# Every second block of u multiplied as plain float32 while the heads are routed, and the tokens scaled in place

## The chip, the core and the metric

The kernel runs on one core of one Trainium2 chip. The metric is the device time of one execution in microseconds (us). A core has five engines with a queue of instructions each: TensorE (PE, with its weight loads shown as PEld), VectorE (DVE), ScalarE (ACT), GpSimd (POOL) and SyncE (SP), which here only issues DMAs. Each queue runs in its own order; semaphores make an instruction wait for another engine.

## What is computed

Two transformer-like blocks on 256 tokens of width 1024. The change lies in the last part, the expert layer of the second block (PEER):

```python
q = (xf @ w_q).reshape(n_tok, 8, 256)                      # 8 heads, keys of 2 x 128
s1 = einsum("thd,hnd->thn", q[..., :128], sub_keys[:, 0])  # and s2 with the other half
v1, i1 = top_k(s1, 16); v2, i2 = top_k(s2, 16)             # routing: 16 experts a head and token
idx, gates = ...top_k(v1 + v2)..., softmax(vals)
act = gelu(einsum("chkd,cd->chk", u[idx], xc))             # u: 16384 x 1024
out = einsum("chk,chkd->cd", act * gates, v[idx])
```

The kernel does not gather for most tokens: it multiplies all 16384 rows of u with 224 of the 256 tokens, in 128 blocks of 128 experts, and spreads the gates over the experts. The last 32 tokens (`GT`) are done by fetching the chosen rows of u and v.

## The kernel before

Products that must be as exact as float32 are made of three matmuls in the reduced form fp32r (`mm3`, line 209): an operand is split into a rounded part (hi, made by an ACT cast) and its remainder (lo, by a subtraction on DVE or POOL), and hi·hi, hi·lo and lo·hi are added up in PSUM.

The part at issue, in program order:

- `finish` (lines 1062 to 1074) adds the last residual to `h` and makes `hT`, the tokens transposed (128 x 1024 for each of two tiles c of 128 tokens), times a gain, but not yet times each token's scale `r4[c]`, which `row_scale` computes meanwhile on ACT and POOL.
- `scores(c, hd)` (lines 1236 to 1249): 16 plain float32 matmuls of `hT[c]` with the head's query weights (line 1241), 4 records of line 1247 with the sub keys, and an ACT copy that multiplies by `r4[c]`. A plain float32 matmul appears in the trace as two MATMUL records.
- Lines 1255 to 1262: the scaled tokens `t` are made on DVE from `hT` and a PSUM tile that holds r4 along the free side (`over_free`, line 318), then split into `x3` (`xuh`, `xul`).
- Lines 1264 to 1273: `hg`, the rows of the last 32 tokens, four copies of each, by one DVE operation on 128 x 1024 and two plain float32 matmuls with 512 columns (line 1272).
- `load_e` (lines 1279 to 1290) loads one block of u into a tile `er` (three of these, 512 KB each), casts its halves to `eh` on ACT (line 1286) and makes the remainders `el` (line 1288) on DVE and POOL in turn (`OPT["ulo"]`) until routing is over, and then on DVE alone (`ulo2`). There are four tiles each of `eh` and `el`, two blocks' worth.
- The loop over the 128 blocks (line 1366 on): 8 x `mm3` with 224 columns into `us`, gelu by ACT into `W`. At every fourth block `choose` routes one head of one token tile, a chain of some 30 small DVE operations whose last but one is line 1133, and `scores` makes the scores of a head three or four further on. From the fifth routed head, `fetch` (POOL, line 1322) brings 128 chosen rows of u and `take` (DVE, line 1329) multiplies them with `hg`. When all heads are routed, `weights` makes the gates, and `spread` (lines 1337 to 1360) puts them into `W`.
- For token tile 1, a route ends with a small DMA of the indices (`gidx`, line 1137) in SP's queue, the queue that also issues all loads of `er`.

A scheduler that works from a model of the engines puts the instructions of each engine in their final order; names with a number (`rt_5316`) are tiles.

Of the kernel before, what the change touches and what calls it, by code (L numbers as in the profile page):

```python
# [17 lines left out]
FT = mybir.dt.float32  # L18
# [5 lines left out]
AF = mybir.ActivationFunctionType  # L24
OP = mybir.AluOpType
AX = mybir.AxisListType

P = 128
T = 256
D = 1024  # L30
KT = D // P
# [5 lines left out]
GT = 32  # L37
ND = T - GT
# [7 lines left out]
TILED = ("w_in", "w_out", "w_ple_proj", "w_mlp_up", "w_mlp_down", "w_ple_gate", "w_in_2", "w_out_2", "peer_w_q_2")  # L46
DBG = None
MARK = None
PRI = dict(mix=20000, tail=20000, wt=20000, chain=20000, taps=20000, evac=40000, route=20000)
OPT = dict(lo='VVG', olo='V', mlo='V', clo='G', ulo='VG', ulo2='V', vlo='V', spr='SV', eraw=3, ring1=4, ring2=2, stag=3)  # L50


# [19 lines left out]
def body(ctx: ExitStack, tc: tile.TileContext, A, out, plan):  # L72
    nc = tc.nc
    V, S, G, PE = nc.vector, nc.scalar, nc.gpsimd, nc.tensor
# [22 lines left out]
    def bc(ap, n):  # L97
        return bass.AP(tensor=ap.tensor, offset=ap.offset, ap=[[0, P], [1, n]])
# [4 lines left out]
    scratch = pool(ctx, "scratch", 2)  # L103
# [15 lines left out]
    h = []  # L119
    for c in range(2):  # L120
        t = resid.tile([P, D], FT, name=f"h{c}")
        h.append(t)

    ident = consts.tile([P, P], FT, name="ident")
# [12 lines left out]
    def mm(shape=(P, 512)):  # L137
        return pmm.tile(list(shape), FT, name="mm", tag="mm")
# [67 lines left out]
    def mm3(ps, a, b, start, stop):  # L206

        for i, (x, y) in enumerate(((a[0], b[0]), (a[0], b[1]), (a[1], b[0]))):
            r = PE.matmul(ps, x, y, start=start and i == 0, stop=stop and i == 2)  # L209
        return r  # L210
# [105 lines left out]
    def over_free(r_, np_=P, c0=0, ps=None):  # L316

        return PE.matmul(ps[:, c0:c0 + np_], r_[:np_].to_broadcast([np_, P]), ident[:np_, :np_], start=True, stop=True)
# [4 lines left out]
    def over(ap, n=4):  # L323
        return ap[:, None, :].to_broadcast([P, n, P])
# [3 lines left out]
    def rows_(c):  # L328
        return slice(c * P, (c + 1) * P)
# [401 lines left out]
    with ExitStack() as mx:  # L731
# [29 lines left out]
        for c in C:  # L761
            ps = pacc.tile([P, 2, 512], FT, name=f"dn{c}")
# [473 lines left out]
    def scores(c, hd):  # L1236
        qh = scratch.tile([P, 2, P], FT, name="qh", tag="sq")
        ps = mm((P, 2, P))
        for b in range(2):
            for k in range(KT):  # L1240
                PE.matmul(ps[:, b, :], wq[hd](k, rows_(b)), hT[c][:, k, :], start=k == 0, stop=k == KT - 1)  # L1241
        S.copy(qh, ps)
        ps = mm((P, 2, P))
        sc = sc_[:, nsc[0] % 4]
        nsc[0] += 1
        for s in range(2):
            PE.matmul(ps[:, s, :], qh[:, s, :], skT[:, hd * 2 + s, :], start=True, stop=True)
        S.activation(sc, ps, AF.Copy, scale=r4[c])
        return sc

    order = [(1, hd) for hd in (0, 1, 2, 4, 6, 3, 5, 7)] + [(0, hd) for hd in (2, 4, 6, 3, 5, 7)]
    sc1 = [scores(*order[n]) for n in range(2)]


    for c, n in ((0, P), (1, ND - P)):
        ps = mm()
        over_free(r4[c], ps=ps)
        t = eraw.tile([P, KT, P], FT, name="er", tag="er")
        V.tensor_tensor(t, hT[c], over(ps[:, :P], KT), op=OP.mult)
        ts = slice(c * P, c * P + n)  # L1260
        S.copy(x3[0][:, :, ts], t[:, :, :n])
        V.tensor_tensor(x3[1][:, :, ts], t[:, :, :n], x3[0][:, :, ts].bitcast(FT), op=OP.subtract)

    hg = pr.tile([P, D], FT, name="hg")
    hn = eraw.tile([P, D], FT, name="er", tag="er")
    nc.sync.dma_start(hn, bc(A["norm_ffn_g_2"], D))
    V.scalar_tensor_tensor(hn, h[1], r4[1], hn, op0=OP.mult, op1=OP.mult)
    sel = scratch.tile([P, P], FT, name="sel", tag="sq")
    V.tensor_copy(sel.rearrange("p (b t) -> p b t", t=GT), ident[:, None, P - GT:].to_broadcast([P, 4, GT]))
    for n in range(2):  # L1270
        pt = mm()
        PE.matmul(pt, sel, hn[:, n * 512:(n + 1) * 512], start=True, stop=True)
        S.copy(hg[:, n * 512:(n + 1) * 512], pt)
    ag, gg = pr.tile([P, 32], FT, name="ag"), pr.tile([P, 32], FT, name="gg")
    sc1 += [scores(*order[n]) for n in range(2, 4)]

    ne = [0]

    def load_e(src, i, pat):

        raw = eraw.tile([P, D], FT, name="er", tag="er")
        nc.sync.dma_start(raw, src)
        hi, lo = [[esplit.tile([P, 512], FR, name="e" + x, tag="e" + x) for _ in range(2)] for x in "hl"]
        for n in range(2):
            r_ = raw[:, n * 512:(n + 1) * 512]
            S.copy(hi[n], r_)  # L1286
            e = V if pat[ne[0] % len(pat)] == "V" else G
            e.tensor_tensor(lo[n], r_, hi[n].bitcast(FT), op=OP.subtract)  # L1288
            ne[0] += 1
        return hi, lo  # L1290
# [69 lines left out]
            S.copy(W[:, at:, ts], ip[:, at:, :])  # L1360

    mark("u")
    uq = [load_e(A["u"][0], 0, OPT["ulo"])]
    p1 = None
    nr, nsp, nf, ps = 0, 0, 0, None
    for i in range(NB):
        p_ = i // 2
        if i + 1 < NB:
            uq.append(load_e(A["u"][i + 1], i + 1, OPT["ulo"] if p1 is None else OPT["ulo2"]))
        uh, ul = uq.pop(0)  # L1370
        if i % 2 == 0:
            ps = pu.tile([P, 2, T], FT, name="us", tag="us")[:, :, :ND]
        for k in range(KT):
            ks = rows_(k % 4)
            mm3(ps[:, i % 2, :], (uh[k // 4][:, ks], ul[k // 4][:, ks]), (x3[0][:, k, :], x3[1][:, k, :]), k == 0, k == KT - 1)
        if i % 2 == 0:
            continue
        ib = slice(i - 1, i + 1)
        nt = 4 * nsp
        if nt < ND:  # L1380
            S.activation(W[:, ib, nt:], ps[:, :, nt:], AF.Gelu_apprx_tanh)
        if nt:
            g_ = scratch.tile([P, 2, T], FT, name="ga", tag="sq")
            S.activation(g_[:, :, :nt], ps[:, :, :nt], AF.Gelu_apprx_tanh)
            V.tensor_tensor(W[:, ib, :nt], W[:, ib, :nt], g_[:, :, :nt], op=OP.mult)
        if nr >= 5 and p_ < 26 or p1 is not None and (todo or nf < 32):
            if len(todo) == 2 or nf == 32 and todo:
                take()
            if nf < min(32, 16 if nr < 8 else 32):
                fetch("peer_u_2", nf)  # L1390
                nf += 1
        if p_ == 25:
            while todo:
                take()
        if nr < len(order) and p_ % 2 == 0:
            choose(*order[nr], sc1[nr])
            nr += 1
            if nr + 3 < len(order):
                sc1.append(scores(*order[nr + 3]))
            if nr == len(order):  # L1400
                weights()
                more_rows()
                p1 = p_ + 1
        elif nr == len(order):
            want = -(-ND // 4 * (p_ + 1 - p1) // (64 - p1))
            while nsp < want:
                spread(nsp, i + 1, OPT["spr"][nsp % len(OPT["spr"])])
                nsp += 1
# [106 lines left out]
```

## Time and profile before

| | us |
|---|---|
| median of 3 runs | 1417.33 (1414.58 to 1418.09) |
| the profiled execution | 1420.28 |
| its span, first to last instruction | 1418.4 |
| mean granted TensorE clock | 0.974 of full |
| routing and u, first score to the last product of u | 563.27 to 1067.92 |

The profiled execution is 2.95 us above the median, and 1.9 us of it lie outside the span. The stage at issue covers 505 us, 36% of the span; the v products follow it.

### The profile page before, as it was taken

Reading aid. Unit: us, or ns where it says so; the run is one execution under the profiler, and the core shown is the slowest. Engines: PE = TensorE matmul, PEld = TensorE weight load, DVE = VectorE, ACT = ScalarE, POOL = GpSimd, SP = SyncE. Lnnn points to the kernel's source line nnn. Section 1 sums busy time; section 2 is a strip of 40 time slices with the busy share of each in tenths; the row PEclk is TensorE's granted clock in tenths of the full one; section 3 lists DMA queues with packets and bytes.
Section 4 is the critical chain, followed back from the end, with each engine's and each line's share of the span. In section 5 each row is a group of like instructions: output and inputs, shape, how many; then the busy total and the mean of one; then the engine's idle time right before and its main releaser. Section 6 shows DMA issues by size and latency. Waiting matters only on the chain.

```text
span 1418.4 us, 25628 instructions
## 1 busy us (share of the span) xinstructions
PE 1325.7 (93%) x9602; PEld 1250.2 (88%) x9602; DVE 1085.3 (77%) x2205; ACT 745.8 (53%) x1422; POOL 295.2 (21%) x278
## 2 busy tenths in 40 slices
PE   5999999999998969698899899999999999999997
PEld 5989979998878958598899899999998899899997
DVE  4978948765557986889987977888886676777765
ACT  5785356444454433243444566776665554555554
POOL 2520012000004851136434620000000121221000
PEclk9999999999999979899999999999999999999999
DMA  7533045655636500738546884544456778777773
GB/s 268 167 122 120 19 168 197 200 183 186 189 117 224 177 15 3 281 113 290 164 157 192 290 263 156 161 161 155 151 165 196 249 267 271 270 262 256 218 210 116
DMA packets 72780, 261.30 MB, mean 184 GB/s; under 512 B 9024, under 2 KB 9408, under 8 KB 71760
## 3 DMA queue, kind: packets, MB, share of 16 engines
q1 hardware_dynamic: 62432, 224.82, 48.1%
q0 software_dynamic: 9216, 33.56, 7.3%
q8 instruction: 75, 1.23, 0.4%
q10 hardware_dynamic: 1008, 1.30, 0.3%
q14 instruction: 49, 0.40, 0.1%
HBM read 258.56 MB, written 1.05 MB: 183 GB/s over the span
## 4 chain that ended last, share of the span: by engine, by line
PE 69%; DVE 18%; DMA 7%; ACT 3%; issue 3%; POOL 0%; ACTq 0%; DVEq 0%; POOLq 0%
PE us L209 18%; PE mm L209 18%; PE dn L209 6%; PE vacc L1437 5%; PE mm L1437 5%; DMA er<-in_peer_v_dram 4%; DVE el L1288 4%; PE mm L1355 3%; PE vacc L1435 3%; PE mm L1435 2%; DVE cfp L1024 2%; PE mm L1241 2%; ACT eh L1286 1%; DMA rows<-in_peer_u_dram,gidx 1%; DVE cv L390 1%
## 5 line engine op out<-in xcount | busy, mean ns | idle before, releaser
L1286 ACT CAST eh<-er 128x512 fp32r<-128x512 f32 x512 | 311.1, 619 | 331.1 <-PE us L209 141.1
L1288 DVE TENSOR_TENSOR el<-er,eh 128x512 fp32r<-128x512 f32 x457 | 321.7, 724 | 133.0 <-ACT eh L1286 131.0
L209 PE MATMUL us<-xuh,el 128*128 128x224 f32 x1024 | 284.7, 278 | 18.8 <-DVE el L1288 12.9
L209 PE MATMUL us<-xuh,eh 128*128 128x224 f32 x1024 | 288.0, 281 | 1.8 <-ACT eh L1286 1.8
L209 PE MATMUL us<-xul,eh 128*128 128x224 f32 x1024 | 283.4, 277 | 0.0
L209 PEld LDWEIGHTS us<-xuh,el 128*128 128x128 f32 x1024 | 198.9, 194 | 22.2 <-DVE el L1288 15.4
L193 ACT CAST wh<-w 128x1024 fp32r<-128x1024 f32 (+1 forms) x142 | 147.7, 1050 | 130.5 <-PE mm L209 75.6
L209 PEld LDWEIGHTS us<-xuh,eh 128*128 128x128 f32 x1024 | 199.2, 194 | 2.1 <-ACT eh L1286 2.1
L199 DVE TENSOR_TENSOR wl<-w,wh 128x1024 fp32r<-128x1024 f32 (+1 forms) x110 | 135.4, 1237 | 84.3 <-ACT wh L193 84.1
L209 PEld LDWEIGHTS us<-xul,eh 128*128 128x128 f32 x1024 | 199.2, 195 | 0.0
L1437 PE MATMUL vacc<-w,eh 128*128 128x448 f32 x508 | 167.2, 375 | 0.0
L1437 PE MATMUL mm<-w,eh 128*128 128x448 f32 x508 | 167.2, 375 | 0.0
L1435 PE MATMUL vacc<-w,el 128*128 128x224 f32 x512 | 137.8, 269 | 4.9 <-DVE el L1288 4.4
L1322 POOL DMA_INDIRECT rows<-in_peer_v_dram,gidx x32 | 49.0, 1532 | 428.6 <-DVE hg L1331 248.7
L1435 PE MATMUL mm<-w,el 128*128 128x224 f32 x512 | 135.5, 265 | 0.0
L209 PE MATMUL mm<-xTh,wh 128*128 128x256 f32 x416 | 118.9, 286 | 14.0 <-ACT wh L193 13.9
L209 PE MATMUL mm<-xTl,wh 128*128 128x256 f32 x416 | 118.6, 285 | 0.6 <-DVE xTl L253 0.6
L209 PE MATMUL mm<-xTh,wl 128*128 128x256 f32 x416 | 118.4, 285 | 0.0
L1435 PEld LDWEIGHTS vacc<-w,el 128*128 128x128 f32 x512 | 98.0, 191 | 11.2 <-DVE el L1288 11.0
L203 POOL TENSOR_TENSOR wl<-w,wh 128x512 fp32r<-128x512 f32 (+1 forms) x64 | 87.2, 1389 | 83.7 <-ACT wh L193 83.6
L1437 PEld LDWEIGHTS mm<-w,eh 128*128 128x128 f32 x508 | 95.3, 188 | 7.2
L1437 PEld LDWEIGHTS vacc<-w,eh 128*128 128x128 f32 x508 | 95.5, 188 | 6.8
(421 smaller groups left out, 2800.1 us busy)
## 6 DMA issues: line engine op xcount, KB each, us to landing
er<-in_u_dram SPq DMA_DIRECT2D x128, 512.0 KB
er<-in_peer_v_dram SPq DMA_DIRECT2D x128, 512.0 KB
w<-in_w_in_dram SPq DMA_DIRECT2D x48, 512.0 KB
w<-in_w_mlp_up_dram SPq DMA_DIRECT2D x32, 512.0 KB
w<-in_w_mlp_down_dram SPq DMA_DIRECT2D x32, 512.0 KB
w<-in_w_out_dram SPq DMA_DIRECT2D x16, 512.0 KB
W<-in_peer_w_q_dram SPq DMA_DIRECT2D x6, 1024.0 KB
w<-in_w_ple_gate_dram SPq DMA_DIRECT2D x8, 512.0 KB
```

The source lines that it names most:

```text
L193: S.copy(hi, t)
L199: V.tensor_tensor(lo, t, hi.bitcast(FT), op=OP.subtract)
L203: G.tensor_tensor(lo[s_], t[s_], hi[s_].bitcast(FT), op=OP.subtract)
L209: r = PE.matmul(ps, x, y, start=start and i == 0, stop=stop and i == 2)
L1024: V.scalar_tensor_tensor(cf[:, b, :] if k == 30 else part, uc[:, b, k:k + T], wk_, part, op0=OP.mult, op1=OP.add)
L1241: PE.matmul(ps[:, b, :], wq[hd](k, rows_(b)), hT[c][:, k, :], start=k == 0, stop=k == KT - 1)
L1286: S.copy(hi[n], r_)
L1288: e.tensor_tensor(lo[n], r_, hi[n].bitcast(FT), op=OP.subtract)
L1322: G.indirect_dma_start(out=rw, out_offset=None, in_=A[name][0], in_offset=bass.IndirectOffsetOnAxis(ap=gidx[:, n % 32:n % 32 + 1], axis=0))
L1355: PE.matmul(ps[:, k, :], wj[:, k, :], one[:, k, :], start=True, stop=True)
L1435: PE.matmul(acc[b][:, :ND], vl[n][:, bs], wi[:, :ND], start=False, stop=False)
L1437: PE.matmul(acc[b], vh[n][:, bs], wi, start=False, stop=i == NB - 1)
```

## The change

1. Blocks 0, 2, 4, ... 50 of u are no longer split: their raw tile `er` is the weight operand of 8 plain float32 matmuls with 224 columns of `hT` (new line 1378).
2. The other blocks are as before, but all their remainders are made on DVE: POOL has none left.
3. The scaled tokens are written over `hT` itself, under a priority `xu` (new lines 1253 to 1260); the scores are taken from the scaled `hT`, so their copy no longer scales.
4. The rows `hg` (`by_rows`) are made after block 9 and no longer ahead of block 0.

```diff
-        S.activation(sc, ps, AF.Copy, scale=r4[c])
+        S.copy(sc, ps)
...
-    sc1 = [scores(*order[n]) for n in range(2)]
-
-
-    for c, n in ((0, P), (1, ND - P)):
-        ps = mm()
-        over_free(r4[c], ps=ps)
-        t = eraw.tile([P, KT, P], FT, name="er", tag="er")
-        V.tensor_tensor(t, hT[c], over(ps[:, :P], KT), op=OP.mult)
-        ts = slice(c * P, c * P + n)
-        S.copy(x3[0][:, :, ts], t[:, :, :n])
-        V.tensor_tensor(x3[1][:, :, ts], t[:, :, :n], x3[0][:, :, ts].bitcast(FT), op=OP.subtract)
+
+    with tc.high_priority(offset=PRI["xu"]):
+        for c, n in ((0, P), (1, ND - P)):
+            ps = mm()
+            over_free(r4[c], ps=ps)
+            V.tensor_tensor(hT[c], hT[c], over(ps[:, :P], KT), op=OP.mult)
+            ts = slice(c * P, c * P + n)
+            S.copy(x3[0][:, :, ts], hT[c][:, :, :n])
+            V.tensor_tensor(x3[1][:, :, ts], hT[c][:, :, :n], x3[0][:, :, ts].bitcast(FT), op=OP.subtract)
+    sc1 = [scores(*order[n]) for n in range(4)]
...
-    def load_e(src, i, pat):
+    def load_e(src, i, pat, exact=False):
 
         raw = eraw.tile([P, D], FT, name="er", tag="er")
         nc.sync.dma_start(raw, src)
+        if exact:
+            return raw, None
...
-            uq.append(load_e(A["u"][i + 1], i + 1, OPT["ulo"] if p1 is None else OPT["ulo2"]))
+            uq.append(load_e(A["u"][i + 1], i + 1, OPT["ulo2"], p1 is None and i + 1 < 52 and (i + 1) % 4 in (0, 2)))
...
+            if ul is None:
+                PE.matmul(ps[:, i % 2, :], uh[:, rows_(k)], hT_[:, k].rearrange("p c t -> p (c t)")[:, :ND], start=k == 0, stop=k == KT - 1)
+                continue
             mm3(ps[:, i % 2, :], (uh[k // 4][:, ks], ul[k // 4][:, ks]), (x3[0][:, k, :], x3[1][:, k, :]), k == 0, k == KT - 1)
...
+        if p_ == 4:
+            by_rows()
```

How the queues stand there. On PE at the start of u, before: the scores of two heads (lines 1241 and 1247), the two rows of r4 (line 318), the product for hg (line 1272), a third head, then block 0 as fp32r.

```order
L1241 MATMUL mm<-hT,wq 128x128 x16
L1247 MATMUL mm<-skT,qh 128x128 x2
L1241 MATMUL mm<-hT,wq 128x128 x16
L1247 MATMUL mm<-skT,qh 128x128 x2
L318 MATMUL mm<-ident,r_5513 128x128
L318 MATMUL mm<-ident,r_5624 128x128
L1272 MATMUL mm<-er,sel 128x512 x2
L1241 MATMUL mm<-hT,W 128x128 x16
L209 MATMUL us<-xuh,eh 128x224
```

The same place after the change; line 1066 is the transposes of `finish`, line 1378 the plain products of u.

```order
L1066 MATMUL mm<-ident,h_86 128x128 x5
L318 MATMUL mm<-ident,r_5513 128x128
L1066 MATMUL mm<-ident,h_86 128x128 x3
L318 MATMUL mm<-ident,r_5624 128x128
L1241 MATMUL mm<-hT,wq 128x128 x16
L1378 MATMUL us<-hT,er 128x224 x8
L209 MATMUL us<-xuh,eh 128x224
L209 MATMUL us<-xul,eh 128x224
L1378 MATMUL us<-hT,er 128x224 x2
L1247 MATMUL mm<-skT,qh 128x128 x2
```

The rows of r4 have moved ahead of the first score, the first block of u stands behind that score, and line 1272 (now 1274) is gone from here.

On DVE ahead of the first score, after the change: the second route (lines 1104 to 1114, on `rt`) with the scaling (line 1257, second tile) in its middle and the split (line 1260) behind it.

```order
L1108 MAX_INDEX rt_5316<-rt_5316 128x8
L1114 TENSOR_TENSOR rt_5316<-rt_5316 128x120
L1108 MAX_INDEX rt_5316<-rt_5316 128x8
L1113 TENSOR_SCALAR rt_5316<-rt_5316 128x16
L1257 TENSOR_TENSOR hT<-hT,mm 128x8x128
L1104 MAX rt_5316<-rt_5316 128x8
L1105 MAX_INDEX rt_5316<-rt_5316 128x8
L1106 MATCH_REPLACE rt_5316<-rt_5316 128x136
L1260 TENSOR_TENSOR xul<-hT,xuh 128x8x96
```

Before, the scaling stood one route later, behind the same line 1104 of the third route; all of the second route's rows up to line 1133 were ahead of it.

On POOL from the first block of u, before: remainders of u (line 1288) and fetches (line 1322) mixed.

```order
L1149 COPY r_5624<-rr 128x1
L1288 TENSOR_TENSOR el<-er,eh 128x512 x9
L1322 DMA W<-in_peer_u_dram,gidx 128x1024 x4
L1288 TENSOR_TENSOR el<-er,eh 128x512 x2
L1322 DMA W<-in_peer_u_dram,gidx 128x1024 x3
L1288 TENSOR_TENSOR el<-er,eh 128x512
```

After: the fetches alone.

```order
L1149 COPY r_5624<-rr 128x1
L1324 DMA W<-in_peer_u_dram,gidx 128x1024 x17
L1324 DMA rows<-in_peer_u_dram,gidx 128x1024 x8
L1324 DMA rows<-in_peer_v_dram,gidx 128x1024
L1324 DMA rows<-in_peer_u_dram,gidx 128x1024 x2
```

No remainder is left on POOL, so a fetch stands behind fetches only.

## Rows read from the trace of the kernel before

**Rows 1.** The page, busy time of three engines, with share of the span and instructions.

```profile
PE 1325.7 (93%) x9602; PEld 1250.2 (88%) x9602; DVE 1085.3 (77%) x2205; ACT 745.8 (53%) x1422; POOL 295.2 (21%) x278
```

**Rows 2.** Busy time by stretch: PE, PEld, DVE, ACT, POOL, then granted clock, DMA share, GB/s.

```profile
563.27:594.65 31.38, 16.97 (x113) 13.93 (x113) 30.49 (x117) 8.64 (x18) 3.63 (x6) 0.78 0.73 283
594.65:834.16 239.51, 217.44 (x1834) 213.47 (x1832) 211.69 (x585) 103.87 (x194) 116.25 (x88) 0.96 0.62 205
834.16:1067.92 233.76, 233.52 (x2089) 233.33 (x2090) 196.42 (x459) 158.82 (x393) 1.15 (x1) 1.00 0.51 164
```

**Rows 3.** Timeline of PE around the start of u (start, duration, instruction).

```profile
563.27 0.49 PE L1241 MATMUL mm<-hT,wq 128*128 128x128 f32 x2
...
574.13 0.61 PE L318 MATMUL mm<-ident,r 128*128 128x128 f32 x4
587.67 3.65 PE L1272 MATMUL mm<-er,sel 128*128 128x512 f32 x4 [12.93 <-DVE er L1267]
591.16 3.73 PE L1241 MATMUL mm<-hT,W 128*128 128x128 f32 x32
```

**Rows 4.** Timeline of PE, first block of u and the next head's scores.

```profile
594.95 0.27 PE L209 MATMUL us<-xuh,el 128*128 128x224 f32 x1
...
597.29 0.28 PE L209 MATMUL us<-xuh,el 128*128 128x224 f32 x1
597.40 0.61 PE L1247 MATMUL mm<-skT,qh 128*128 128x128 f32 x4
597.86 3.74 PE L1241 MATMUL mm<-hT,W 128*128 128x128 f32 x32
601.35 0.35 PE L209 MATMUL us<-xuh,eh 128*128 128x224 f32 x1
```

**Rows 5.** PE in 594.65 to 834.16 by line: busy, mean ns, idle before and releasers.

```profile
L209 PE MATMUL us<-xuh,el 128*128 128x224 f32 x464 | 131.7, 285 | 18.6 <-DVE el L1288 12.6 <-POOL el L1288 5.9
...
L1241 PE MATMUL mm<-hT,W 128*128 128x128 f32 x355 | 44.2, 282 | 0.0
```

**Rows 6.** Timeline of DVE ahead of the first block of u.

```profile
562.86 0.35 DVE L1073 TENSOR_SCALAR hT<-mm,cols 128x128 f32<-128x128 f32 x1 [0.31 <-PE mm L1066]
563.13 0.48 DVE L1104 MAX8 rt<-rt 128x8 f32<-128x128 f32 x2
...
566.44 0.22 DVE L1113 TENSOR_SCALAR rt<-rt 128x16 f32<-128x16 f32 x1
...
570.87 0.69 DVE L1133 TENSOR_REDUCE keys<-rt 128x32 f32<-128x512 f32 x1
...
574.61 2.33 DVE L1259 TENSOR_TENSOR er<-hT,mm 128x1024 f32<-128x1024 f32 x2
...
577.14 1.21 DVE L1262 TENSOR_TENSOR xul<-er,xuh 128x1024 fp32r<-128x1024 f32 x1
```

**Rows 7.** DVE in 594.65 to 834.16 by line.

```profile
L1288 DVE TENSOR_TENSOR el<-er,eh 128x512 fp32r<-128x512 f32 x60 | 57.6, 965 | 10.2 <-ACT eh L1286 9.8
L1329 DVE CUSTOM_DVE_ANT_0 W<-W,hg 128x1024 f32<-128x1024 f32 x17 | 26.2, 1544 | 5.3 <-DMA W<-in_peer_u_dram,gidx 5.3
```

**Rows 8.** DVE in 900 to 1000 by line, where POOL has no remainders.

```profile
L1288 DVE TENSOR_TENSOR el<-er,eh 128x512 fp32r<-128x512 f32 x60 | 40.6, 688 | 11.2 <-ACT eh L1286 11.0
```

**Rows 9.** POOL in 594.65 to 834.16 by line.

```profile
L1288 POOL TENSOR_TENSOR el<-er,eh 128x512 fp32r<-128x512 f32 x53 | 74.8, 1418 | 77.4 <-ACT eh L1286 73.8 <-PE us L209 3.2
```

**Rows 10.** Timeline of DVE and of POOL, two takes and two remainders.

```profile
638.14 3.80 DVE L1329 CUSTOM_DVE_ANT_0 W<-W,hg 128x1024 f32<-128x1024 f32 x1 [4.43 <-DMA W<-in_peer_u_dram,gidx]
...
642.96 1.21 DVE L1329 CUSTOM_DVE_ANT_0 W<-W,hg 128x1024 f32<-128x1024 f32 x1
...
638.36 2.49 POOL L1288 TENSOR_TENSOR el<-er,eh 128x512 fp32r<-128x512 f32 x2
```

**Rows 11.** Timeline of SP and of ACT, one load of u and the cast that waited for it.

```profile
648.84 0.33 SPq L1282 DMA_DIRECT2D er<-in_u_dram  x1
...
654.25 1.18 ACT L1286 CAST eh<-er 128x512 fp32r<-128x512 f32 x2 [2.37 <-DMA er<-in_u_dram]
```

More of the change, by code (lines that the diff above doesn't have):

```diff
@@ L48 @@
 MARK = None
-PRI = dict(mix=20000, tail=20000, wt=20000, chain=20000, taps=20000, evac=40000, route=20000)
+PRI = dict(mix=20000, tail=20000, wt=20000, chain=20000, taps=20000, evac=40000, xu=20000, route=20000)
 OPT = dict(lo='VVG', olo='V', mlo='V', clo='G', ulo='VG', ulo2='V', vlo='V', spr='SV', eraw=3, ring1=4, ring2=2, stag=3)
@@ L1264, in body @@
-    hg = pr.tile([P, D], FT, name="hg")
[L1265 to L1273, printed above, removed]
+    with tc.high_priority(offset=PRI["xu"]):
[6 more added lines that the diff above has]
+            V.tensor_tensor(x3[1][:, :, ts], hT[c][:, :, :n], x3[0][:, :, ts].bitcast(FT), op=OP.subtract)
@@ new lines, in body, with by_rows @@
+    sc1 = [scores(*order[n]) for n in range(4)]
+    hg = pr.tile([P, D], FT, name="hg")
+    def by_rows():
+        hn = eraw.tile([P, D], FT, name="er", tag="er")
+        nc.sync.dma_start(hn, bc(A["norm_ffn_g_2"], D))
+        V.scalar_tensor_tensor(hn, h[1], r4[1], hn, op0=OP.mult, op1=OP.mult)
+        sel = scratch.tile([P, P], FT, name="sel", tag="sq")
+        V.tensor_copy(sel.rearrange("p (b t) -> p b t", t=GT), ident[:, None, P - GT:].to_broadcast([P, 4, GT]))
+        for n in range(2):
+            pt = mm()
+            PE.matmul(pt, sel, hn[:, n * 512:(n + 1) * 512], start=True, stop=True)
+            S.copy(hg[:, n * 512:(n + 1) * 512], pt)
@@ L1274, in body @@
     ag, gg = pr.tile([P, 32], FT, name="ag"), pr.tile([P, 32], FT, name="gg")
-    sc1 += [scores(*order[n]) for n in range(2, 4)]
     ne = [0]
-    def load_e(src, i, pat):
+    def load_e(src, i, pat, exact=False):
         raw = eraw.tile([P, D], FT, name="er", tag="er")
         nc.sync.dma_start(raw, src)
+        if exact:
+            return raw, None
         hi, lo = [[esplit.tile([P, 512], FR, name="e" + x, tag="e" + x) for _ in range(2)] for x in "hl"]
@@ L1362, in body @@
     mark("u")
-    uq = [load_e(A["u"][0], 0, OPT["ulo"])]
+    uq = [load_e(A["u"][0], 0, OPT["ulo"], True)]
     p1 = None
```

## Prediction

> **What bounds the kernel now.** I began with the page: PE is busy 93% of the span [rows 1], so one looks for where it is not. The busy time by stretch shows that it is not in two places of the stage at issue [rows 2]: between the first score and the first product of u (16.97 of 31.38 us, clock 0.78), and while heads are routed (217.44 of 239.51, clock 0.96). From 834.16 on PE is busy 233.52 of 233.76 at full clock, and there only less work for PE would help; the change leaves that work as it is.
>
> The start, from the timeline [rows 3, 4]. A head's scores take 601.35 - 597.40 = 3.95 us of PE. Three heads less one closing product, 3 x 3.49 + 2 x 0.46 = 11.4, is all that u needs in these 31.4 us. The other 20.0 are 12.93 of waiting for the rows of hg, 3.5 for their product (two records of each matmul, at half clock), the rows of r4 and small waits.
>
> The routing. A block of u is 24 records; the 3rd to the 24th start 597.29 - 594.95 = 2.34 apart, 0.1114 each, 2.68 a block. 58 blocks make 155.4; the scores 355/32 = 11.1 heads of 3.95, 43.8 [rows 5]. With some 5 us of other products that stay (four spreads, the transposes of the gates) the work is 204 of 239.5, so about **35 us are waits and half clock**. PE's own waits name the remainders, on DVE and on POOL [rows 5]. DVE is nearly always occupied (211.69 of 239.51 [rows 2]), but not with its own work alone: a remainder on DVE takes 965 ns here and 688 in a later stretch where POOL has none [rows 7, 8]; a take that met two remainders of POOL took 3.80 us instead of 1.21 [rows 10]. DVE and POOL exclude one another there. In the remainders and the first 17 takes alone DVE loses 60 x 0.277 + 17 x (1.544 - 1.21) = 22.3 us, to 53 remainders of 74.8 us on POOL [rows 7, 9].
>
> **The change, part by part.**
>
> *Plain products.* [...] **26 x 0.47 = +12.2 us** of PE (8 to 16).
> [...]
>
> *Casts and remainders that go.* 52 casts on ACT (busy 103.87 of 239.51) save nothing by themselves. DVE keeps as many remainders, two for every second block in place of one for each. POOL's go, and with them the 22 us or more of exclusion on DVE. That is the gain of the routing stage: per four blocks and a score PE now needs 2 x 2.68 + 2 x 3.15 + 3.95 = 15.6, while DVE needs a route, 8.4 (571.56 - 563.13, with three short evictions in it [rows 6]), and four remainders of 0.69, 11.2. So PE sets the pace, but not where takes come thick. Behind the fifth of token tile 1's heads some 16 takes of 1.21 fall on three routes: 3 x 8.4 + 14 x 0.69 + 16 x 1.21 = 54 us on DVE against 3 x 15.6 = 47 on PE. DVE starts with a lead, since POOL's delay is gone; I leave 8 us of waiting there. The other takes, now behind the last route with the first spreads, I give 5, and 3 go to loads that come late (below). **35 - 16 = 19 us come back** (12 to 27).
>
> *The start.* In place scaling puts 1.17 + 1.21 (half of 2.33, and a split [rows 6]) among the transposes' evictions and the route, and the second 1.17 ahead of the first score. From 562.86 to the end of line 1113 DVE took 3.8; with 3.6 more the first score starts near 570.3 instead of 563.27. PE idles some 5 us there, and may run its first score at half clock: 7.0 + 1.8 lost. Behind it block 0 needs no split: its raw tile is loaded long before, since no `t` and no hn sits in the three raw tiles. The 20.0 of now shrink to 8.8; the product for hg comes later at full clock, 1.8. **20.0 - 8.8 - 1.8 = 9.4 us come back** (6 to 13).
>
> *Edits at nothing.* The copy without scale is one ACT operation as before. hn's 1.27 on DVE and `sel` move behind block 9, under PE's slack. Three loads of u now go ahead of weights of an earlier stage on SP; I see no wait for a DMA on PE there and take 0 (up to 3 lost). DVE's routes start later by the score's delay, some 9 us, but are not what PE waits for until the takes.
>
> **The sum**, on the profiled execution: 1420.28 + 12.2 - 19 - 9.4 = 1404. It is 2.95 over the median, so the forecast is **1401 us**, 16 faster.
>
> **Rivals.**
>
> 1. *Everything behind PE.* If takes and loads hide wholly, and plain products cost 3.04, the sum is +9.4 - 32 - 9.4: 32 faster, 1385. For it: DVE's own work, 211.69 less 22, leaves 50 us in the stage. Against it: 16 takes cannot spread out before their routes. 13%.
> 2. [...] 13%.
> 3. *DVE's chain sets the routing whatever POOL does.* Routes with takes ended as late for want of fetched rows: 16 of 512 KB and 14 blocks of u in some 50 us are 300 GB/s, more than the 283 of the busiest stretch shown [rows 2]. Then only some 5 of the 35 come back, and with +12.2 and -9.4 the sum is 1420.28 - 2.2, or 1415 against the median. For it: the first 17 takes waited 5.3 us for their DMA [rows 7]. 9%.
> 4. *Slower: the raw tiles.* A plain block holds its tile until its last product, so the load for the block three further on starts only then, and that block is split. Load to cast was 5.4 us for a load that a cast waited for [rows 11], then cast and remainder, 0.59 + 0.69, 6.7 in all; PE has 2.68 + 3.15 = 5.83 till it wants them, 9.8 where a score lies between. Also each index DMA stands among these loads on SP and waits for its route. If every one of 26 such blocks waited 1.5 us, 39 us would be lost: 1437. It decides from 16/26 = 0.6 us each. Against it: that load was in the thickest fetches, and half of the gaps have a score. 10%.
>
> **How the numbers follow.** The forecast has 55%, with a range of its own of 1393 to 1409 (its three bounds, partly cancelling). A change of under 0.3%, 4.3 us, could not be told from none. Faster: the forecast, rival 1, most of 2: 0.81. Same: rival 3 and the edge of 2: 0.09. Slower: rival 4: 0.10. The range 1385 to 1416 leaves out rival 4 and a few per cent beyond rival 1.
>
> **What would show it.** Right: POOL with no remainder in the stage; DVE's remainder near 0.69 and its take near 1.21 throughout; plain records 0.19 to 0.205 apart; first product of u near 574 and last near 1050; waits of PE for remainders mostly in the three routes with takes. Wrong: plain records 0.22 apart or more; casts waiting for loads of u at every second block; PE's idle in the routing stage above 20 us; the first score later than 573.

## The result, and the profile after

The changed kernel took 1397.53 us (median of 4 runs, 1396.03 to 1399.99), the kernel before 1417.71 us beside it (4 runs, 1414.58 to 1422.57): a ratio of 0.9856, 95% interval 0.9824 to 0.9889. The forecast was 1401. The profiled execution took 1398.40 us, its span is 1396.6 us.

The page's busy times (answers to [rows 1]):

```profile
PE 1324.4 (95%) x9394; PEld 1252.7 (90%) x9394; DVE 1041.2 (75%) x2208; ACT 711.0 (51%) x1370; POOL 214.1 (15%) x223
```

Busy time by stretch (columns as in [rows 2]); the last product of u now starts at 1049.27 and no longer at 1067.78:

```profile
563.27:594.65 31.38, 25.25 (x187) 24.82 (x186) 25.22 (x102) 10.47 (x21) 1.11 (x4) 0.89 0.68 269
594.65:834.16 239.51, 228.17 (x1715) 223.78 (x1714) 187.80 (x639) 81.58 (x175) 38.86 (x36) 0.99 0.61 214
834.16:1049.60 215.44, 215.44 (x1931) 215.44 (x1931) 181.96 (x426) 145.10 (x359) 0.00 (x0) 1.00 0.50 163
```

In the same routing stretch PE's gaps fell from 22.1 to 11.3 us, its clock rose from 0.96 to 0.99, and DVE does 24 us less. PE at the start, with a product of line 1046 that all kernels here share, and one plain block later on (answers to [rows 3, 4]):

```profile
524.55 2.93 PE L1046 MATMUL st<-cf,mean 128*128 128x128 f32 x12 [9.35 <-DVE cf L1024]
...
565.64 0.49 PE L318 MATMUL mm<-ident,r 128*128 128x128 f32 x2 [1.68 <-POOL r L1149]
570.58 5.46 PE L1241 MATMUL mm<-hT,wq 128*128 128x128 f32 x32 [4.46 <-DVE hT L1257]
575.87 3.19 PE L1378 MATMUL us<-hT,er 128*128 128x224 f32 x16
...
599.34 3.20 PE L1378 MATMUL us<-hT,er 128*128 128x224 f32 x16
602.38 0.61 PE L1247 MATMUL mm<-skT,qh 128*128 128x128 f32 x4
```

The first score waits 4.46 us for the scaling and runs for the most part at half clock (granted 0.50 in 570.58 to 573.50, 0.68 in 570.58 to 575.87; 5.29 us to the next product, 3.49 before). A plain block needs 602.38 - 599.34 = 3.04 us, 0.190 for each of its 16 records.

PE, DVE and POOL by line in 594.65 to 834.16 (answers to [rows 5], [rows 7] and [rows 9]; lines 1288, 1290, 1324 and 1331 were 1286, 1288, 1322 and 1329):

```profile
L209 PE MATMUL us<-xuh,eh 128*128 128x224 f32 x285 | 83.5, 293 | 4.8 <-ACT eh L1288 4.8
L209 PE MATMUL us<-xuh,el 128*128 128x224 f32 x283 | 79.7, 281 | 2.3 <-DVE el L1290 2.1
...
L1378 PE MATMUL us<-hT,er 128*128 128x224 f32 x384 | 76.8, 353 | 0.0
```

```profile
L1290 DVE TENSOR_TENSOR el<-er,eh 128x512 fp32r<-128x512 f32 x71 | 47.2, 684 | 24.6 <-ACT eh L1288 21.8 <-PE us L209 2.8
L1331 DVE CUSTOM_DVE_ANT_0 W<-W,hg 128x1024 f32<-128x1024 f32 x17 | 20.7, 1218 | 7.7 <-DMA er<-in_u_dram 4.2 <-DMA W<-in_peer_u_dram,gidx 3.5
```

```profile
L1324 POOL DMA_INDIRECT W<-in_peer_u_dram,gidx x17 | 18.0, 1056 | 104.6 <-ACT eh L1288 68.5 <-DMA gg<-keys 17.3 <-DVE ag L1331 5.6
L1324 POOL DMA_INDIRECT rows<-in_peer_u_dram,gidx x15 | 16.1, 1073 | 113.3 <-issue 76.4 <-DVE ag L1331 30.3 <-DVE oh L1354 6.6
```

PE waits for DVE's remainders 2.1 us where it waited 12.6, none for POOL's, but 4.8 for casts. DVE's remainder takes 684 ns (965 before), its take 1218 (1544). POOL has fetches alone.

**A common clock.** Executions differ by up to 3.7 us in the part that all kernels here share. So the table below counts from the product of line 1046 (524.55 above, 524.09 before): to the first score, to the first and the last product of u; then from the last product of u to the end of the span. "Start": old, new (as changed), or in place (scaling over `hT`, but at its old place in the program). "Lo": who makes the remainders while heads are routed. The ratio is the timed one against the kernel before, with its 95% interval. The other columns are of one execution each, and executions of one kernel differ by up to 11 us (f2: 1387.75 to 1398.62), so a difference of a few us between two rows is firm only where the ratios differ too.

| run | start | lo | plain blocks | raw tiles | first score | first u | last u | behind | ratio |
|---|---|---|---|---|---|---|---|---|---|
| before | old | DVE, POOL | 0 | 3 | 39.2 | 70.6 | 543.7 | 350.7 | 1 |
| changed | new | DVE | 26 | 3 | 46.0 | 51.3 | 524.7 | 347.4 | 0.9856 (0.9824 to 0.9889) |
| e1 | new | DVE, POOL | 0 | 3 | 46.0 | 51.5 | 535.0 | 350.1 | 0.9916 (0.9889 to 0.9943) |
| e2 | in place | DVE | 26 | 3 | 39.2 | 56.8 | 518.9 | 349.1 | 0.9811 (0.9782 to 0.9841) |
| e3 | new | DVE | 0 | 3 | 46.0 | 51.6 | 518.3 | 347.0 | 0.978 (0.975 to 0.981) |
| e4 | new | DVE, POOL | 26 | 3 | 46.0 | 51.6 | 537.3 | 349.8 | 0.9928 (0.9901 to 0.9954) |
| f1 | old | DVE | 0 | 3 | 39.2 | 70.3 | 524.3 | 347.6 | 0.9844 (0.9818 to 0.987) |
| f2 | in place | DVE | 0 | 3 | 39.2 | 57.9 | 516.7 | 348.1 | 0.981 (0.9782 to 0.9839) |
| f3 | in place | DVE, POOL | 0 | 3 | 39.2 | 58.2 | 535.4 | 348.4 | 0.9922 (0.9896 to 0.9949) |
| e5 | new | DVE | 26 | 4 | 46.0 | 51.8 | 521.1 | 339.5 | 0.9738 (0.9712 to 0.9764) |
| e8 | new | DVE | 52 | 3 | 46.0 | 51.5 | 528.1 | 346.3 | 0.9858 (0.9832 to 0.9884) |
| h4 | old | DVE, POOL | 0 | 4 | 40.7 | 72.4 | 545.7 | 339.8 | 0.992 (0.9896 to 0.9945) |
| h1 | new | DVE | 0 | 4 | 46.0 | 51.5 | 516.1 | 339.7 | 0.9704 (0.9675 to 0.9733) |
| h2 | in place | DVE | 0 | 4 | 39.1 | 57.9 | 512.6 | 339.5 | 0.9685 (0.966 to 0.971) |

The changed kernel's 21.8 us of span are 19.0 up to the last product of u, 3.3 behind it, less 0.5 ahead of line 1046.

### The profile page after: what moved, and what is told of

Read it like the earlier page. It is cut to its first block, busy times and chain, and to the rows that moved or that the text cites. A ratio compares the mean times of both kernels' runs of the same rounds, so it can differ in the third digit from the quotient of the medians.

```text
span 1396.6 us, 24993 instructions
## 1 busy us (share of the span) xinstructions
PE 1324.4 (95%) x9394; PEld 1252.7 (90%) x9394; DVE 1041.2 (75%) x2208; ACT 711.0 (51%) x1370; POOL 214.1 (15%) x223
## 4 chain that ended last, share of the span: by engine, by line
PE 69%; DVE 15%; DMA 9%; ACT 3%; issue 3%; POOL 1%; ACTq 0%; DVEq 0%; POOLq 0%; SPq 0%
PE mm L209 18%; PE us L209 15%; PE dn L209 6%; PE vacc L1444 5%; PE mm L1444 5%; DMA er<-in_peer_v_dram 4%; PE mm L1357 3%; DVE el L1290 3%; DMA er<-in_u_dram 3%; PE vacc L1442 3%; PE us L1378 2%; PE mm L1442 2%; PE mm L1241 2%; DVE cfp L1024 2%; ACT eh L1288 1%
## 5 line engine op out<-in xcount | busy, mean ns | idle before, releaser
L1288 ACT CAST eh<-er 128x512 fp32r<-128x512 f32 x460 | 277.5, 619 | 322.0 <-DMA er<-in_u_dram 82.1
L1290 DVE TENSOR_TENSOR el<-er,eh 128x512 fp32r<-128x512 f32 x460 | 305.9, 687 | 142.2 <-ACT eh L1288 137.8
L209 PE MATMUL us<-xuh,eh 128*128 128x224 f32 x816 | 231.7, 284 | 4.8 <-ACT eh L1288 4.8
L209 PE MATMUL us<-xuh,el 128*128 128x224 f32 x816 | 227.2, 278 | 2.3 <-DVE el L1290 2.1
L209 PE MATMUL us<-xul,eh 128*128 128x224 f32 x816 | 223.3, 274 | 0.0
L209 PEld LDWEIGHTS us<-xuh,eh 128*128 128x128 f32 x816 | 157.2, 193 | 6.4 <-ACT eh L1288 6.4
L209 PEld LDWEIGHTS us<-xuh,el 128*128 128x128 f32 x816 | 157.3, 193 | 3.8 <-DVE el L1290 3.6
L209 PEld LDWEIGHTS us<-xul,eh 128*128 128x128 f32 x816 | 157.4, 193 | 0.0
```

## The experiments

The theory at first: the start and POOL's remainders give time back, each by itself, plain products cost PE some, and DVE needs their relief to do without POOL. The rival: the plain products are beside the point, or even the whole gain comes from one part.

**e1, the start alone.** Every block split, remainders on DVE and POOL in turn. Against the changed kernel:

```diff
-    uq = [load_e(A["u"][0], 0, OPT["ulo"], True)]
+    uq = [load_e(A["u"][0], 0, OPT["ulo"])]
...
-            uq.append(load_e(A["u"][i + 1], i + 1, OPT["ulo2"], p1 is None and i + 1 < 52 and (i + 1) % 4 in (0, 2)))
+            uq.append(load_e(A["u"][i + 1], i + 1, OPT["ulo"] if p1 is None else OPT["ulo2"]))
```

> The changed start alone: tokens scaled in place, rows hg after block 9; every block of u split, remainders on DVE and POOL in turn as before. My theory takes the start as a term of its own: 9 to 11 us faster than before (about 1408), first score at 570.6, first product of u near 576, and DVE's remainders in the routing stage still near 0.95 us because POOL's are back. Rival (the routing stage swallows it: DVE's chain of routes, now later, and its slow remainders set when u ends, whenever u begins): 0 to 4 us faster, with PE's waits for remainders longer than the 18.6 us of before by what the start gave.

1407.9 us as expected, 0.9916; the last product of u 8.7 us earlier. The start is a term of its own and the routing stage does not swallow it. DVE's remainders are slow again (its lines in 594.65 to 834.16):

```profile
L1290 DVE TENSOR_TENSOR el<-er,eh 128x512 fp32r<-128x512 f32 x67 | 59.8, 899 | 8.4 <-ACT eh L1288 6.7 <-PE us L209 1.5
L1331 DVE CUSTOM_DVE_ANT_0 W<-W,hg 128x1024 f32<-128x1024 f32 x17 | 26.2, 1544 | 0.0
```

**e2, plain products, with the scaling at its old place.** The tokens are still scaled in place, but behind two scores, and `hg` stands ahead of block 0:

```diff
-    with tc.high_priority(offset=PRI["xu"]):
-        for c, n in ((0, P), (1, ND - P)):
+    sc1 = [scores(*order[n], scaled=False) for n in range(2)]
+    for c, n in ((0, P), (1, ND - P)):
...
-    sc1 = [scores(*order[n]) for n in range(4)]
...
+    by_rows()
+    sc1 += [scores(*order[n]) for n in range(2, 4)]
...
-        if p_ == 4:
-            by_rows()
```

> Plain products for every second block and remainders on DVE alone, but the start as before the change (first two scores from the unscaled tokens, scaling and rows hg ahead of block 0). My theory: plain products cost 9.4 us (records 0.190 apart), POOL's absence gives back 16.5, so 7 us faster than before (about 1410), with DVE's remainder at 0.69 and its take at 1.21. Rival (the plain products only pay because the start moved; without it the two terms cancel): within 3 us of before. Rival of the other side (most of the gain is here, little in the start): 14 us or more faster.

1393.29 us, 0.9811: the other side's rival by its number. But the run was not what its name says, since its start lost little: PE's timeline has no wait for the rows of `hg`, and the DVE operation behind them, at 586.25 before, ran at 564.32.

```profile
572.92 0.61 PE L318 MATMUL mm<-ident,r 128*128 128x128 f32 x4
573.36 1.88 PE L1276 MATMUL mm<-er,sel 128*128 128x512 f32 x4
576.01 3.84 PE L1241 MATMUL mm<-hT,W 128*128 128x128 f32 x32 [0.76 <-DVE hT L1260]
579.68 3.19 PE L1382 MATMUL us<-hT,er 128*128 128x224 f32 x16
```

So with the scaling in place the 12.93 us wait of [rows 3] is gone at its old place in the program too, and this start comes without the 4.46 us of the changed one. f3 below tests it alone.

**e3, no plain products, all remainders on DVE.**

```diff
-    uq = [load_e(A["u"][0], 0, OPT["ulo"], True)]
+    uq = [load_e(A["u"][0], 0, OPT["ulo2"])]
...
-            uq.append(load_e(A["u"][i + 1], i + 1, OPT["ulo2"], p1 is None and i + 1 < 52 and (i + 1) % 4 in (0, 2)))
+            uq.append(load_e(A["u"][i + 1], i + 1, OPT["ulo2"]))
```

> The change without its plain products: every block split, all remainders on DVE, none on POOL. My theory (DVE must be relieved by the plain blocks): PE saves 9.4 us of work, but DVE gets 52 remainders of 0.69 more, 36 us, in a stage where it was busy 188 of 240; per four blocks and a head DVE then needs 8.4 + 8 x 0.69 = 13.9 against PE's 14.7, and the 21 us of takes come on top: 5 to 15 us slower than the changed kernel (1403 to 1413). Rival (POOL's absence is all that counts): 9 us faster than the changed kernel, 1388.

1388.88 us, 0.978, where the changed kernel has 0.9856: my theory that DVE needs the relief fell. PE's waits in 563 to 834 (engine and line, then the releaser; us, times, longest):

```profile
PE us L209 <- DVE el L1290: 7.0, 7, 1.8
PE mm L1241 <- DVE hT L1257: 4.4, 1, 4.4
PE us L209 <- ACT eh L1288: 4.2, 4, 1.6
```

DVE is busy 218.5 of 239.5 us in the routing stretch, with 127 remainders, and PE still waits for it only 7.0. The plain products add 9.4 us of work to PE and save less than that: with them the last product of u comes 6.4 us later.

**e4, POOL's remainders back in the split blocks.**

```diff
-            uq.append(load_e(A["u"][i + 1], i + 1, OPT["ulo2"], p1 is None and i + 1 < 52 and (i + 1) % 4 in (0, 2)))
+            uq.append(load_e(A["u"][i + 1], i + 1, OPT["ulo"] if p1 is None else OPT["ulo2"], p1 is None and i + 1 < 52 and (i + 1) % 4 in (0, 2)))
```

> The changed kernel, but the remainders of the split blocks in the routing stage alternate between DVE and POOL again (26 on each). My theory (DVE and POOL exclude one another): DVE's mean remainder goes from 0.685 back towards 0.9 and takes above 1.4; DVE has 26 remainders (18 us) less, but POOL's own take 1.4 each, so PE waits 4 to 10 us more, 1402 to 1408. Rival (exclusion doesn't matter, DVE's load does): 3 us faster than the changed kernel or the same, with PE's waits for remainders shorter than 5.7 us.

1410.72 us, 0.9928, the last product of u 12.6 us later than in the changed kernel: slower as expected, and by more. But not by the way I gave: DVE's remainder takes 700 ns and its take 1304, hardly more than the 684 and 1218 without, and PE waits for DVE's remainders 3.0 us (2.1). DVE's small operations are slower again (line 1113 takes 457 ns, 217 in the changed kernel), but PE's new waits are others. The timelines of ACT, POOL, DVE and PE show another way:

```profile
627.40 0.61 ACT L1288 CAST eh<-er 128x512 fp32r<-128x512 f32 x1
```

```profile
631.58 1.72 POOL L1324 DMA_INDIRECT W<-in_peer_u_dram,gidx  x1 [20.47 <-DVE rt L1107]
...
636.09 0.94 POOL L1324 DMA_INDIRECT W<-in_peer_u_dram,gidx  x1 [0.30 <-issue]
637.05 1.27 POOL L1290 TENSOR_TENSOR el<-er,eh 128x512 fp32r<-128x512 f32 x1
```

```profile
636.69 2.73 DVE L1331 CUSTOM_DVE_ANT_0 W<-W,hg 128x1024 f32<-128x1024 f32 x1 [2.60 <-issue]
```

```profile
638.38 0.37 PE L209 MATMUL us<-xuh,el 128*128 128x224 f32 x1 [2.31 <-POOL el L1290]
...
640.00 4.46 PE L1378 MATMUL us<-hT,er 128*128 128x224 f32 x16
```

The cast was done at 628.0. The remainder stands on POOL behind four fetches, of which the first starts only at 631.58, after a route's index DMA that SP issued at 628.96, so it starts at 637.05, and PE waits 2.31 us. Then PE's clock falls, by the windows (columns as in [rows 2]):

```profile
638.40:639.03 0.63, 0.63 (x5) 0.63 (x6) 0.63 (x1) 0.00 (x0) 0.00 (x0) 1.00 0.92 358
639.03:641.00 1.97, 1.97 (x10) 1.90 (x9) 1.83 (x9) 0.00 (x0) 0.95 (x1) 0.52 0.86 337
```

The next plain block takes 4.29 us to the following product (640.00 to 644.29) and not 3.04. Over the routing stretch PE waits 6.3 us for POOL's remainders and 3.7 for loads of u, neither of which it does in the changed kernel, and its clock is 0.97 (0.99). A remainder on POOL is thus late by its place in the queue as well. The take at 636.69 shows the exclusion too: it took 1.51 us more than its usual 1.22, with POOL's 1.27 us remainder inside it. Why the take lost time though it started first, 0.36 us ahead of the remainder, the profile does not show.

**f1, one letter.** The kernel before with all remainders on DVE.

```diff
-OPT = dict(lo='VVG', olo='V', mlo='V', clo='G', ulo='VG', ulo2='V', vlo='V', spr='SV', eraw=3, ring1=4, ring2=2, stag=3)
+OPT = dict(lo='VVG', olo='V', mlo='V', clo='G', ulo='V', ulo2='V', vlo='V', spr='SV', eraw=3, ring1=4, ring2=2, stag=3)
```

> The kernel before with one letter changed: all remainders of u on DVE, none on POOL; no plain products, old start. If what counts in the routing stage is only that POOL has no remainders (as the run with all blocks split says), the gain is the difference of that run and of the one with the start alone, 25.4 - 8.7 from the first common instruction to the last product of u: 17 us faster than before, ratio 0.988. Rival (the remainders fit on DVE only because the new start gave DVE a lead): 5 us faster or less, with PE's waits for DVE's remainders above 12.9 us.

1397.15 us, 0.9844: as fast as the changed kernel. The last product of u is 19.4 us earlier. The routing stretch by time and by DVE's lines, beside [rows 2] and [rows 7]:

```profile
594.65:834.16 239.51, 228.14 (x1999) 225.49 (x1998) 214.58 (x680) 118.38 (x232) 41.14 (x36) 0.99 0.64 222
```

```profile
L1288 DVE TENSOR_TENSOR el<-er,eh 128x512 fp32r<-128x512 f32 x127 | 85.2, 682 | 7.9 <-ACT eh L1286 7.4
L1329 DVE CUSTOM_DVE_ANT_0 W<-W,hg 128x1024 f32<-128x1024 f32 x17 | 20.6, 1216 | 8.2 <-DMA W<-in_peer_u_dram,gidx 8.2
L1113 DVE TENSOR_SCALAR rt<-rt 128x16 f32<-128x16 f32 x12 | 2.6, 218 | 0.0
```

Line 1113 in the kernel before, and then PE's waits for DVE's remainders in f1 ([rows 5] has them before):

```profile
L1113 DVE TENSOR_SCALAR rt<-rt 128x16 f32<-128x16 f32 x12 | 6.7, 557 | 0.0
```

```profile
PE us L209 <- DVE el L1288: 7.7, 8, 2.5
```

DVE makes 127 remainders where it made 60, with 12 routes in the stretch as before, and is busy 214.58 us instead of 211.69: POOL's half of the remainders had cost DVE almost as much time as doing them. At the mean times of f1, line by line, DVE's operations of that stretch before come out some 43 us shorter (an estimate from the two traces): 17 of it in remainders, 6 in the first 17 takes, and the rest in small operations like line 1113, which the prediction did not count. PE's waits for remainders fall from 18.5 us (12.6 for DVE's and 5.9 for POOL's) to 7.7.

**f2 and f3, the scaling in place at its old place, without plain products.** The start of e2; in f2 the remainders are on DVE (the edit of e3), in f3 on DVE and POOL in turn (the edit of e1).

> Tokens scaled in place but at their old place behind two scores, rows hg ahead of block 0, every block split, all remainders on DVE, no plain products. If the order of the start (worth 5.9 us between the run with plain products alone and the changed kernel) and the lack of plain products (6.4 us) add up: 31 us faster than before, ratio 0.978, 12 us faster than the changed kernel. Rival (both took the same waits away): no better than the run with all blocks split, 25 us faster.

> Only the scaling in place, at its old place in the order; rows hg ahead of block 0, every block split, remainders on DVE and POOL in turn. My theory now: the 12.93 us wait for the rows of hg came from the raw tiles that the scaled tokens held, so in place scaling alone removes it: first score where it was before, the product for hg without a wait, first product of u 13 to 17 us earlier; 14 us faster than before, ratio 0.990. Rival (the wait was DVE's order, not the tiles): the product for hg still waits over 8 us, 3 us faster or less.

f2 took 1393.01 us, 0.981, its last product of u 27.0 us earlier than before (in a profiled execution 5.3 us under the median): near the rival. The better start of e2 and the lack of plain products do not add up; e2 and f2 are alike in ratio. f3 took 1409.66 us, 0.9922, with the last product of u 8.3 us earlier: the first product of u came 12.4 us earlier (13 to 17 expected), and the routing stage, with POOL's remainders, took 4 back. The wait for the rows of `hg` is gone (0.80 us is left, for `sel`). That the raw tiles caused it is tested by h4.

**e5, four raw tiles.** The changed kernel; room comes from a small tile with one buffer less.

```diff
-OPT = dict(lo='VVG', olo='V', mlo='V', clo='G', ulo='VG', ulo2='V', vlo='V', spr='SV', eraw=3, ring1=4, ring2=2, stag=3)
+OPT = dict(lo='VVG', olo='V', mlo='V', clo='G', ulo='VG', ulo2='V', vlo='V', spr='SV', eraw=4, ring1=4, ring2=2, stag=3)
...
-            sm = small.tile([P, 8], FT, name="sm8", bufs=2)
+            sm = small.tile([P, 8], FT, name="sm8", bufs=1)
```

> The changed kernel with four raw tiles of u and not three. If plain blocks cost more than their products because they hold a raw tile until their last matmul, so that loads, casts and PE wait: ACT's casts wait for loads half as long as the 82 us of the changed kernel, PE's waits for casts go from 4.8 to under 2 us, and the time falls by 3 to 6 us. Rival (those casts have slack, PE's waits have another cause, such as takes): ACT's waits fall but the time stays within 2 us.

1383.35 us, 0.9738: about three times the expected gain, two thirds of it elsewhere. Up to the last product of u it is 3.6 us: PE no longer waits for casts, though ACT waits for loads of u nearly as long (first with three tiles, then with four, 570 to 820), where I had expected half.

```profile
ACT eh L1288 <- DMA er<-in_u_dram: 79.6, 20, 9.1
```

```profile
ACT eh L1288 <- DMA er<-in_u_dram: 68.5, 17, 8.2
```

The 3.6 us are a net of two things. Up to block 52, where the stretch with plain blocks ends, u is 7.3 us ahead of the changed kernel (259.5 and 266.8 us on the common clock). 3.7 of these are lost again behind it, where a remainder on DVE stands behind a take that waits for its row:

```profile
789.75 0.56 PE L209 MATMUL us<-xuh,el 128*128 128x224 f32 x1 [5.16 <-DVE el L1290]
```

```profile
787.86 1.23 DVE L1331 CUSTOM_DVE_ANT_0 rows<-rows,hg 128x1024 f32<-128x1024 f32 x1 [4.36 <-DMA rows<-in_peer_u_dram,gidx]
```

The other 7.9 us lie behind the last product of u, in the v stage, which uses the same tiles. ACT and PE there, 1060 to 1340, first with three tiles (the changed kernel), then with four:

```profile
ACT eh L1288 <- DMA er<-in_peer_v_dram: 72.3, 41, 3.6
...
PE vacc L1442 <- DVE el L1290: 3.5, 13, 0.7
```

```profile
ACT eh L1288 <- PE mm L1444: 62.4, 104, 0.6
ACT eh L1288 <- PE vacc L1444: 41.1, 94, 0.6
ACT eh L1288 <- DMA er<-in_peer_v_dram: 10.5, 15, 1.1
```

With three tiles the casts wait for loads and PE for the remainders behind them; with four the casts wait for PE. PE's waits that the profile lists are only 3.5 us; in these 280 us PE runs 1729 matmul records with three tiles and 1789 with four, at a clock of 1.00 in both.

**h4, four raw tiles in the kernel before** (the edit of e5).

> The kernel before with four raw tiles and nothing else changed (the scaled tokens still take two of them for a while). If the 12.93 us wait for the rows of hg came from the raw tiles, it goes, and 8 us in the v stage with it: 14 to 18 us faster, ratio 0.988 to 0.990. Rival (the wait is DVE's order, a whole route ahead of the rows): the wait stays at 10 us or more, only the v stage gains: 8 us faster, 0.994.

1407.74 us, 0.992, the rival's number. All of it is behind the last product of u (10.9 us), which itself comes 2.0 us later. The wait for `hg` stayed, as PE's and DVE's timelines show:

```profile
587.33 3.75 PE L1272 MATMUL mm<-er,sel 128*128 128x512 f32 x4 [12.94 <-DVE er L1267]
```

```profile
582.10 0.69 DVE L1133 TENSOR_REDUCE keys<-rt 128x32 f32<-128x512 f32 x1
585.92 1.27 DVE L1267 SCALAR_TENSOR_TENSOR er<-h,r,er 128x1024 f32<-128x1024 f32 x1
```

So not the tiles, but the place of line 1267 on DVE, behind a whole route (its end is line 1133) and the beginning of the next, makes the wait. Why the scheduler puts it earlier once the scaling is done in place stays open.

**e8, all of blocks 0 to 51 plain.**

```diff
-            uq.append(load_e(A["u"][i + 1], i + 1, OPT["ulo2"], p1 is None and i + 1 < 52 and (i + 1) % 4 in (0, 2)))
+            uq.append(load_e(A["u"][i + 1], i + 1, OPT["ulo2"], p1 is None and i + 1 < 52))
```

> The changed kernel with all of blocks 0 to 51 as plain products: no cast and no remainder there. PE's work grows by 26 x 0.36 = 9.4 us; DVE and ACT lose 52 remainders and casts. My theory: DVE was no longer what PE waited for, and each raw tile is now held through its 3.04 us of products, so the extra work shows and the waits for loads grow: 9 to 15 us slower than the changed kernel, ratio 0.992 to 0.996, with PE waiting for loads of u directly. Rival (DVE's and ACT's remaining share still cost PE's other waits): 3 us faster to 3 slower than the changed kernel.

1400.15 us, 0.9858: the rival, no different from the changed kernel. The last product of u goes from 518.3 (none plain) over 524.7 (26) to 528.1 (52): +6.4 and +3.4 for 9.4 of work each. So in these executions a set of 26 plain blocks takes 3 and then 6 us of waits and half clock away. PE's largest group in the routing stretch waits 1.1 us for loads; the raw tiles do not fail here either:

```profile
L1378 PE MATMUL us<-hT,er 128*128 128x224 f32 x774 | 151.5, 353 | 1.1 <-DMA er<-in_u_dram 1.1
```

**h1 and h2, what the runs point to**: every block split, remainders on DVE, four raw tiles; h1 with the changed start (e3 and e5 together), h2 with the scaling in place at its old place (f2 and e5 together).

> The new start, every block split, all remainders on DVE, four raw tiles. The fourth tile took 7.9 us from the part behind the last product of u in the changed kernel (347.4 to 339.5), where casts no longer wait for loads of v, and 3.6 from the rest. If the first part belongs to the v stage it comes here too, and if plain products cost 6.4 net: 8 to 11 us faster than the same without the fourth tile, ratio 0.970 to 0.973, 2 to 4 us faster than the changed kernel with four tiles. Rival (plain products pay once their tiles suffice): slower than the changed kernel with four tiles (0.9738).

> As the run before it, but the scaling in place at its old place and rows hg ahead of block 0. The two starts were worth the same within 2 us with three tiles: ratio 0.970 to 0.973. Rival (with loads ahead by a tile, the old place of the scaling is better by the 6.9 us by which its first score comes earlier): 0.967 or less.

h1 took 1377.71 us, 0.9704, as expected: 5.0 us earlier at the last product of u than e5, which has plain products. But at block 52 the two are level (259.3 and 259.5 us): nearly all of the 5.0 lies behind it, where e5 has its 5.16 us wait, and the intervals of the two ratios overlap. With four tiles it is thus not shown that plain products cost time. h2 took 1374.14 us, 0.9685, the best here, between its expectation and its rival: 3.1% under the kernel before, 1.7% under the changed one by the two ratios. Its last product of u is 3.5 us earlier than in h1, but the two intervals overlap. PE's two longest waits there between 560 and the end:

```profile
PE us L209 <- DVE el L1294: 9.7, 7, 3.0
PE vacc L1443 <- DVE w L1437: 2.3, 1, 2.3
```

## Why the prediction was right, point by point

To the last product of u the prediction had +12.2 - 19 - 9.4 = -16.2; measured were -19.0. The steps from the kernel before over e1 and e3 to the changed one are -8.7, -16.7 and +6.4; the last is 9.4 of work less 3.0 of waits. In the prediction's terms that is +9.4 - 19.7 - 8.7.

**Plain products: the step that was mis-sized.** I took 0.47 us more for a plain block than for a split one, 3.15 in all; that was my estimate, and no run shows it. The runs show 0.190 us for a record and 3.04 for a block, 0.36 over the 2.68 of a split one. The work is 26 x 0.36 = 9.4 us, not 12.2. This is the difference of 2.8; the other two terms are off by 0.7 each and cancel. What the trade gives back, which I put at nothing by itself, is 3.0 us of other waits (e3 against the changed kernel), so the net is +6.4 with three tiles. There the part that gives the change its name costs time, and the ratios bear it out (0.978 and 0.9856, intervals apart). In the other pairs, +5.0 with four tiles (h1, e5) and +2.2 with the start of e2 (e2, f2), the intervals overlap and the cost is not shown.

**POOL's remainders gone: right in size**, 19 forecast. The last product of u comes 16.7 us earlier from e1 to e3, 18.7 from f3 to f2, 19.4 from the kernel before to f1. That DVE has room for all remainders once POOL has none is shown by f1, and it loses more to POOL than I counted: some 43 us and not 22.3. e4 adds what I had not seen: a POOL remainder behind fetches is late without any exclusion. f1 takes both away at once, so how the 19.4 divide between them was not measured; before, PE waited 12.6 us for DVE's remainders and 5.9 for POOL's. The 16 us that I left in the stage came out smaller and elsewhere: PE's gaps are 11.3 us at a clock of 0.99, of them 4.8 for casts, 2.9 for the ACT copy `qh` ahead of line 1247 and only 2.1 for DVE's remainders, where I had 8 at the takes.

**The start: right**, 9.4 forecast, 8.7 in e1. The first score came 6.85 us later by the common clock (7.0 forecast) and lost 1.8 at half clock, as worked out. The same gain came from the scaling in place alone (8.3, f3), which leaves the first score where it was: half of the edit, the priority and the later `hg`, bought nothing here. The prediction did not ask whether the wait for `hg` needed that order.

**Edits at nothing: off by 3.3 us** behind the last product of u. That part varies between 346.3 and 350.7 us over the runs with three tiles, lower mostly where POOL has no remainders (350.1 in e1, 347.0 in e3), but 349.1 in e2; its cause was not settled.

**The rivals.** *All behind PE* asked for no waits at all; 6.9 us of PE's waits for casts and remainders are left. Its sum takes 32 us back where hiding all would be 35, or 1382. Rival 2, that plain products cost still more than forecast (1412), fell: the records are 0.190 us apart, where 0.22 or more was to speak for it. *DVE's chain anyway* fell with f1. *Raw tiles* has its mechanism on ACT, which waits 79.6 us for loads, but PE feels 7.3 of it up to block 52 and 3.6 in all (e5) where the rival priced 39: the casts run ahead of PE. Its 1437 has the 3 us taken off that the 19 had already set aside for late loads, which it does not say; without that it is 1440. I looked for that rival in the routing alone; a cost as large, 8 to 11 us, lay in the v stage, in the kernel before already.

**The tests** named ahead came out: no remainder on POOL, 684 and 1218 ns, 0.190 apart, last product of u at 1049. The first product of u is at 575.87, not near 574. PE's waits are mostly for casts, not for DVE, and the casts' wait for loads at many blocks, which I had listed as a sign of being wrong, is there (20 waits) but cost PE no more than the 7.3 us above.

## What to carry to other kernels

When a change couples several edits, price each by itself and ask whether it needs the others: here one letter gave the whole gain (f1, 0.9844), and the most laborious edit, the plain products, lost a part of it (0.9856 with them, 0.978 without). An engine that looks full may be full of somebody else's interference: DVE took over all of POOL's remainders in almost the same busy time (214.58 us for 211.69, f1). How long an engine with slack waits for its buffers is not what they cost: ACT waited 79.6 us for loads in the routing and 72.3 in the v stage, and a fourth tile gave 7.3 us up to block 52 and 7.9 behind u. So read what waits behind a ring of buffers in every stage that shares it.

## What the runs showed of the hardware

A plain float32 record with 224 columns starts 0.190 us after the one before (changed kernel, 599.34 to 602.38), an fp32r record with the same columns 0.1114 [rows 4]. So two plain records took as long as 3.4 fp32r ones, and a block of u 3.04 us in 16 plain records, 2.68 in 24 split ones.

A wait of PE of 2.31 us (e4) was followed, 0.7 us after PE resumed, by a lower granted clock, 0.52 in 639.03 to 641.00 and 0.62 in 641 to 643, then 1.00 again in 643 to 645. The fp32r records from 639.14 on start 0.21 us apart where they were 0.11, and the plain block behind them takes 4.29 us for 3.04. If the clock was half from 639.1 to 642.5, which gives those two means, the 3.4 us lost about 1.7 (an estimate from them), three quarters of the wait's length on top of it. In the kernel before, the product for `hg` ran at a granted 0.51 (587.67 to 591.16) behind its wait of 12.93 us.

While POOL made remainders, some of DVE's operations took longer, small ones among them: the remainder 965 ns for 682, line 1113 on 128 x 16 elements 557 for 218, but line 1107 on 128 x 128 elements 280 for 283 (means in 594.65 to 834.16, before and f1). A remainder on POOL took longer too: one that began 0.11 us after one on DVE took 1.71 us (689.49, before), one beside which DVE ran nothing 1.28 (764.55). Moving POOL's share to DVE raised DVE's busy time by 2.9 us in 239.5.
